# Hybrid decoder layer on one core: masking the decays first, urgent squares and chains, and later first-key products

## The chip, the cores and the metric

The kernel runs on one core of a Trainium2 chip. The metric is device time in microseconds (us), the median of several runs. The profile shows the engines TensorE (PE, with its weight loads PEld), VectorE (DVE), ScalarE (ACT), GpSimd (POOL) and the queue that issues transfers (SP).

## What is computed

One layer on a sequence of 1024 tokens of width 1024. After a norm, one projection gives the columns of two mixers. Mixer A is a gated delta rule with 4 heads of 128 in chunks (the reference's chunk is 64, the kernel's 128); mixer B is dilated window attention with 8 heads of 64. Their outputs are projected and added to the input; a gated MLP with a short convolution and a last norm follow. What the change touches is in mixer A:

```python
qkv_a = jax.nn.silu(causal_dwconv(qkv_a, conv_qkv_w)).astype(jnp.float32)
...
ka = l2norm(ka)
beta = jax.nn.sigmoid(b_a.astype(jnp.float32))
g = -jnp.exp(a_log) * jax.nn.softplus(a_a + dt_bias)
...
gc = jnp.cumsum(chunk_sc(g), axis=-1)
diff = gc[..., :, None] - gc[..., None, :]
dec_incl = jnp.where(incl, jnp.exp(jnp.where(incl, diff, 0.0)), 0.0)
kk = jnp.einsum('nbhtd,nbhjd->nbhtj', kc, kc)
lmat = dec_strict * kk * bc[..., None, :]
...
sol = lax.linalg.triangular_solve(lmat, rhs, left_side=True, lower=True, unit_diagonal=True)
...
def step(state, xs):
    u = uv - jnp.einsum('bhck,bhkv->bhcv', wk, state)
    o = jnp.einsum('bhck,bhkv->bhcv', qd, state) + jnp.einsum('bhcj,bhjv->bhcv', at, u)
    state = ge[..., None, None] * state + jnp.einsum('bhck,bhcv->bhkv', ke, u)
```

## The kernel before

The kernel keeps activations with features on the partitions. A dense product is three matmuls of 128x128x512 on split numbers (`mm3`, with high and low parts), so that a column of 128 output features takes 48 of them. TensorE's order is written by a planner in the kernel, `Weave`: each piece of work is a generator (a stream) with a level; the planner holds an estimated TensorE time `wv.pe` and estimated times at which tiles become ready, takes the stream of the lowest level number among those that are due, and runs it to its next `yield`, whose value says in how many microseconds it wants to go on. `wv.need(tile, slack=...)` is the time until a tile is ready plus a margin; `next_bank("atr")` waits until one of the two result banks of that name is free by the estimates. Each TensorE instruction is stamped, so that TensorE keeps the planner's order exactly. The class `Engine` wraps the other engines: each call adds an estimated duration to the planner's books and then issues the instruction. The order on those engines isn't the planner's; a list scheduler chooses it by readiness and by priority, which follows program order unless it is raised. All their calls pass through one line, so nearly every instruction of VectorE, ScalarE, GpSimd and of the transfer queue has the line L132 in the profile, every matmul L177 and every transpose L181, and groups are told apart by tiles.

The stages, in order of time:

- `first()` multiplies the first three key columns while the input arrives. Beside it, `gates()` multiplies the input by the eight gate columns (`wba`), 8 products for each half, and `norms()` spreads the norm factors `rst` over the partitions into `rstdB` in two halves of transposes. `gates()` ends with the cumulated log decays `gc` and writes them as rows to memory (`gdram`).
- `dense()` multiplies the remaining columns, the fourth key first, then columns of mixer B and the queries and values. It fills whatever the other streams leave free (level 9).
- `first_keys()` and `conv_silu()` turn key columns into keys: three multiply-adds on VectorE, a tanh on ScalarE and a last multiply-add. `kprep(h)` follows for each head: it loads the rows of decays as `dec`, subtracts, masks and exponentiates them, and copies their last column to `gel`; it transposes the keys (`tokens()`, four transposes into each of two `atr` banks), copies them to `ktok` and squares them on ScalarE with a sum for each token (`sq`, sums in `ssk`); and it multiplies keys with keys into `atr` banks, which VectorE takes with `bp` (from `ssk`) and `dec` into `um`.
- After the fourth head, `forward_sub()` solves all 32x32 blocks on VectorE, and `merge()` (two streams of two heads) joins them to 128x128 with small products. `qprep()` and `vprep()` run beside this.
- Four `chain(h)` streams, one for each head, step through eight chunks. A step goes from TensorE to VectorE and back three times: `r`, then `wke`, then the new state (in the tile `ct`), and beside it ScalarE copies `w`, and the output collects in `vtok` with its squares `osq`.
- Attention, output projection, MLP up and down, and the last norm follow. The change doesn't touch them.

The tile for the squares in `tokens()` and the chains has the tag `osq` with one buffer; the tags `w0` to `w3` belong to the chains' `w`. `kprep()` ties `gel` and the decays' first ScalarE pass behind the keys' last operations with order-only dependencies (`after`).

Of the kernel before, what the change touches and what calls it, by code (L numbers as in the profile page):

```python
# [15 lines left out]
P = 128  # L16
# [6 lines left out]
APART = 0.5  # L23
EPS = 1e-6
SLOTS = {"kT": 2, "kU": 2, "dv": 2, "dw": 2, "kt": 4, "uy": 5, "qa": 4, "ev": 2, "go": 2, "Xa": 7, "Xb": 9}
# [91 lines left out]
class Engine:  # L117


    def __init__(self, wv, eng, name, fixed, per, lag=0.28):  # L120
        self.args = wv, eng, name, fixed, per, lag

    def __getattr__(self, op):
        wv, eng, name, fixed, per, lag = self.args

        def call(*a, **kw):
            aps = [x for x in a + tuple(kw.values()) if hasattr(x, "tensor")]
            acc = [kw["accum_out"]] if "accum_out" in kw else []
            n = float(np.prod(aps[0].shape[1:]))
            us = 0.3 + 0.165 * n if kw.get("op") == OP.pow else fixed + per * n  # L130
            wv.account(name, us, aps[:1] + acc, aps[1:], lag)
            return getattr(eng, op)(*a, **kw)  # L132
        return call


def hybrid_layer(tc, I, out):
# [3 lines left out]
    ac = Engine(wv, nc.scalar, "scalar", 0.12, 0.00085)  # L140
    po_ = Engine(wv, nc.gpsimd, "gpsimd", 0.15, 0.0021)
# [191 lines left out]
    def norms():  # L333
        yield wv.need(acc, slack=8.0)
        ssp = yield from next_bank("atr", acc)
        for c in range(NCH):
            mm(ssp[:, c:c + 1], acc[:, c * P:(c + 1) * P], ones[:, :1], 0.215)
            if c % 2:
                yield APART
        ve.tensor_scalar(rst, ssp[:, :NCH], 1.0 / 1024, EPS, op0=OP.mult, op1=OP.add)  # L340
        rsqrt(rst, rst, NCH)
        wv.done.add("rst")
        yield wv.need(rst)
        for h in range(2):
            pb = yield from next_bank("atr")
            for c in range(4):
                i = 4 * h + c
                tp(pb[:, c * P:(c + 1) * P], rst[:, i:i + 1].to_broadcast([P, P]))
            ve.tensor_copy(rstdB[:, half(h)], pb)
        wv.done.add("norms")  # L350
# [154 lines left out]
    def tokens(src, dst, scale=None, ss=None):  # L505

        for hh in range(2):
# [4 lines left out]
            if dst is not None and scale is None:  # L512
                ac.activation(dst[:, half(hh)], pt, AF.Copy)
            for c in range(4):
                i = 4 * hh + c
                if scale is not None:
                    ac.activation(dst[:, i * P:(i + 1) * P], pt[:, c * P:(c + 1) * P], AF.Copy,
                                         scale=scale[:, i:i + 1])
                if ss is not None:
                    sq = tile_(sp, [P, P], F32, "sq", "osq", 1)  # L520
                    ac.activation(sq, pt[:, c * P:(c + 1) * P], AF.Square, accum_out=ss[:, i:i + 1])
        return dst

    def kprep(h):
# [23 lines left out]
        yield wv.need(kT, slack=SLACK)  # L548
# [12 lines left out]
        for c0 in range(0, NCH, 4):  # L561
            pt = yield from next_bank("atr")
# [167 lines left out]
    def chain(h):  # L730
# [14 lines left out]
        for c in range(NCH):  # L745
# [12 lines left out]
            else:  # L758
# [3 lines left out]
                ve.scalar_tensor_tensor(r, ps[:, 0:P], ngam[:, c, h:h + 1], vtok[:, cs], op0=OP.mult, op1=OP.add)  # L762
# [3 lines left out]
            if c < NCH - 1:  # L766
                wke = tile_(sp, [P, P], F32, "wke", "r" + tg, 1)
                ve.tensor_scalar(wke, ps[:, P:2 * P], ke[:, c:c + 1], None, op0=OP.mult)
            ac.activation(w, ps[:, P:2 * P], AF.Copy)
            if c < NCH - 1:  # L770
# [3 lines left out]
                if c == 0:  # L774
                    ve.tensor_copy(sn, ps[:, 2 * P:3 * P])
                else:
                    ve.scalar_tensor_tensor(sn, st, ge[:, c:c + 1], ps[:, 2 * P:3 * P], op0=OP.mult, op1=OP.add)
# [6 lines left out]
            ac.activation(vtok[:, cs], po[:, :P], AF.Copy, scale=rq[:, c:c + 1])  # L784
            if c:
                ve.scalar_tensor_tensor(vtok[:, cs], po[:, P:2 * P], gq[:, c:c + 1], vtok[:, cs], op0=OP.mult,
# [4 lines left out]
            ac.activation(osq, vtok[:, cs], AF.Square, accum_out=ms[:, c:c + 1])  # L791
# [694 lines left out]
```

## Time and profile before

| | us |
|---|---|
| median of 3 runs | 1258.36 |
| lowest, highest | 1257.86, 1259.85 |
| profiled execution | 1259.56 |
| its span | 1257.8 |
| PE busy | 1233.0 |
| DVE busy | 936.0 |
| ACT busy | 621.8 |
| POOL busy | 47.8 |

A timeline row gives start and duration in us, engine, line, operation, output tile and input tiles, the shape, how many instructions are merged, and in square brackets how long the engine had been idle and what ended this. A row of waits gives who waited for whom, the total in us, the number of waits and the longest. Matmuls overlap, so their cost is read from start to start. A matmul of float32 operands is recorded as two instructions, so four products of keys with keys stand as x8.

### The profile page before, as it was taken

How to read it: one execution, taken by the hardware profiler on the slowest of the kernel's cores; microseconds unless marked ns; L12 is line 12 of the kernel's file. 1: busy time of each engine (PE TensorE's matmuls, PEld its weight loads, DVE VectorE, ACT ScalarE, POOL GpSimd, SP SyncE). 2: the span in 40 equal slices, each digit the busy share in tenths (PEclk: the TensorE clock that was granted, in tenths of full speed). 3: DMA queues.
4: the chain of work that ended last, by engine and by line, in shares of the span. 5: the costliest groups of instructions: out<-in, count | busy, mean ns of one | idle time of the engine just before them, and what ended most of it. 6: DMA issues, size and time to landing. Idle time of an engine off the chain costs nothing.

```text
span 1257.8 us, 18320 instructions
## 1 busy us (share of the span) xinstructions
PE 1233.0 (98%) x7040; PEld 1002.1 (80%) x7040; DVE 936.0 (74%) x1462; ACT 621.8 (49%) x1179; POOL 47.8 (4%) x34
## 2 busy tenths in 40 slices
PE   9989999999999999999999999999999999999996
PEld 7768887888676767878788888888888888787886
DVE  7566975563555455676798888888988989899875
ACT  7374444462757374465554454544544454343451
POOL 0021110022000000000000000000000000000000
PEclk9989999999999999999999999999999999999998
DMA  6313244255223420454312313223223298545523
GB/s 228 100 57 94 85 116 137 101 160 206 96 78 100 140 63 26 126 179 139 118 51 101 92 59 101 85 67 101 79 73 101 68 353 290 167 138 198 192 85 134
DMA packets 81974, 153.52 MB, mean 122 GB/s; under 512 B 21824, under 2 KB 32736, under 8 KB 81888
## 3 DMA queue, kind: packets, MB, share of 16 engines
q1 hardware_dynamic: 81888, 152.37, 37.1%
q8 instruction: 55, 0.90, 0.3%
q14 instruction: 31, 0.25, 0.1%
HBM read 114.31 MB, written 35.93 MB: 119 GB/s over the span
## 4 chain that ended last, share of the span: by engine, by line
PE 84%; DVE 7%; DMA 4%; ACT 2%; issue 2%; SPq 0%; POOL 0%; POOLq 0%; DVEq 0%; ACTq 0%
PE ps L177 44%; PE pa L177 18%; PE pc L177 9%; PE dw L177 8%; PE ps L181 4%; DMA wd<-in_wd 3%; DVE pr L132 2%; DVE x1h L132 1%; DVE wd L132 1%; ACT dec L132 1%; DVE kT L132 1%; PE warm L177 1%; DMA wst<-in_wu 0%; DVE r L132 0%; DVE xr L132 0%
## 5 line engine op out<-in xcount | busy, mean ns | idle before, releaser
L177 PE MATMUL dw<-pr 128*128 128x512 f32 (+1 forms) x984 | 213.3, 377 | 2.8 <-DVE x1h L132 2.8
L177 PEld LDWEIGHTS dw<-pr 128*128 128x128 f32 x984 | 176.1, 188 | 38.9 <-DVE x1h L132 4.9
L177 PE MATMUL ps<-xhi,whi 128*128 128x512 f32 x448 | 186.5, 416 | 0.0
L177 PE MATMUL ps<-xhi,wlo 128*128 128x512 f32 x448 | 175.8, 392 | 0.0
L177 PE MATMUL ps<-xlo,whi 128*128 128x512 f32 x448 | 175.3, 391 | 0.0
L177 PE MATMUL pa<-T,pair 128*128 128x512 f32 x528 | 127.1, 389 | 0.6 <-ACT u L132 0.6
L177 PEld LDWEIGHTS pa<-T,pair 128*128 128x128 f32 x528 | 99.0, 188 | 21.1 <-ACT u L132 0.7
L177 PEld LDWEIGHTS ps<-xhi,whi 128*128 128x128 f32 x448 | 84.6, 189 | 19.9 <-issue 6.0
L177 PEld LDWEIGHTS ps<-xhi,wlo 128*128 128x128 f32 x448 | 84.4, 188 | 18.5
L177 PEld LDWEIGHTS ps<-xlo,whi 128*128 128x128 f32 x448 | 84.8, 189 | 13.5
L132 ACT ACTIVATE sm<-sm,mx 128x512 f32<-128x512 f32 (+2 forms) x128 | 79.9, 651 | 23.0 <-DVE mx L132 23.0
L132 ACT ACTIVATE u<-pa 128x512 f32<-128x512 f32 x44 | 26.4, 600 | 110.5 <-PE pa L177 110.5
L132 DVE SCALAR_TENSOR_TENSOR y<-xu,fcw,y 128x1023 f32<-128x1023 f32 (+1 forms) x44 | 56.3, 1281 | 25.7 <-ACT y L132 25.7
L132 ACT ACTIVATE whi<-wst 128x1024 fp32r<-128x1024 f32 (+2 forms) x38 | 38.7, 1017 | 70.4 <-PE ps L177 63.0
L177 PE MATMUL pc<-B,pair 128*128 128x512 f32 x264 | 63.4, 389 | 0.0
L177 PE MATMUL pa<-B,A 128*128 128x512 f32 x264 | 63.4, 389 | 0.0
L177 PE MATMUL pc<-T,S 128*128 128x512 f32 x264 | 63.4, 389 | 0.0
L177 PE MATMUL pa<-T,S 128*128 128x512 f32 x264 | 63.4, 389 | 0.0
L132 ACT ACTIVATE pr<-wd 128x1024 fp32r<-128x1024 f32 x33 | 35.0, 1061 | 55.0 <-DVE wd L132 36.5
L132 DVE TENSOR_TENSOR wst<-wst 128x512 f32<-128x512 f32 x88 | 60.5, 687 | 0.7
L177 PE MATMUL ps<-B,pair 128*128 128x512 f32 x252 | 60.5, 389 | 0.0
L177 PEld LDWEIGHTS pc<-B,pair 128*128 128x128 f32 x264 | 49.6, 188 | 10.3
(230 smaller groups left out, 2279.8 us busy)
## 6 DMA issues: line engine op xcount, KB each, us to landing
wst<-in_wu SPq DMA_DIRECT2D x44, 512.0 KB, 3.7
wd<-in_wd SPq DMA_DIRECT2D x44, 512.0 KB, 4.3
wst<-in_wi SPq DMA_DIRECT2D x25, 512.0 KB, 3.7
upark<-y SPq DMA_DIRECT2D x22, 512.0 KB, 3.7
apark<-aqkv SPq DMA_DIRECT2D x12, 512.0 KB, 2.8
r<-upark SPq DMA_DIRECT2D x11, 512.0 KB, 7.6
r<-upark SPq DMA_DIRECT2D x22, 256.0 KB, 6.7
wa<-in_wd SPq DMA_DIRECT2D x22, 256.0 KB, 2.9
```

The costliest lines, as they stand in the source:

```text
L132: return getattr(eng, op)(*a, **kw)
L177: tc.stamp_issue_order_token(nc.tensor.matmul(dst, lhs, rhs, start=start, stop=stop, **kw).ins, TOKEN)
L181: tc.stamp_issue_order_token(nc.tensor.transpose(dst, src, ident).ins, TOKEN)
```

## The change

- **Decays.** GpSimd's mask (`affine_select`) now comes first, directly on the loaded rows; ScalarE's eight passes by chunk do Exp with the bias instead of Identity, and the separate Exp over 1024 is gone. `gel` is copied after the mask.
- **Priority.** Wrapped engines `uv` and `ua` issue with a priority raised by 400 places. They are used in `tokens()` (copies, scaled copies, squares) and in the four chains.
- **Squares.** The result tiles of the squares in `tokens()` take three tags in turn (`osq`, `w2`, `w3`). The planner's price of a summed Square on ScalarE rises by 0.15 us.
- **Gates.** Each half's eight products are issued in one visit; the pause in the middle moves to the end.
- **Norms.** The second half's spread waits, in the plan, for the first half's copy and 0.3 us.
- **First keys.** For head 0, the transposes are planned 1.5 us later and the first products with themselves 1.0 us later.

```diff
+KSLACK = 1.0
 EPS = 1e-6
+URGENT = 400
...
             us = 0.3 + 0.165 * n if kw.get("op") == OP.pow else fixed + per * n
+            if "func" not in kw and acc and name == "scalar" and a[2] == AF.Square:
+                us += 0.15
             wv.account(name, us, aps[:1] + acc, aps[1:], lag)
-            return getattr(eng, op)(*a, **kw)
+            if first is None:
+                return getattr(eng, op)(*a, **kw)
+            with first(offset=URGENT):
+                return getattr(eng, op)(*a, **kw)
...
+    uv = Engine(wv, nc.vector, "vector", 0.07, 0.00105, first=tc.high_priority)
+    ua = Engine(wv, nc.scalar, "scalar", 0.12, 0.00085, first=tc.high_priority)
...
         for h in range(2):
+            if h:
+                yield wv.need(rstdB, slack=0.3)
             pb = yield from next_bank("atr")
...
                 mm(pt[o:o + 32], wba[:, k, :], xts[k][:, half(h)], 0.23, k < 4, k >= 4, tile_position=(0, o))
-                if k == 3:
-                    yield APART
             ac.activation(barow[:, half(h)], pt, AF.Copy)
-            yield APART
+            yield 2 * APART
...
             if dst is not None and scale is None:
-                ac.activation(dst[:, half(hh)], pt, AF.Copy)
+                ua.activation(dst[:, half(hh)], pt, AF.Copy)
...
                 if ss is not None:
-                    sq = tile_(sp, [P, P], F32, "sq", "osq", 1)
-                    ac.activation(sq, pt[:, c * P:(c + 1) * P], AF.Square, accum_out=ss[:, i:i + 1])
+                    sq = tile_(sp, [P, P], F32, "sq", ("osq", "w2", "w3")[i % 3], 1)
+                    ua.activation(sq, pt[:, c * P:(c + 1) * P], AF.Square, accum_out=ss[:, i:i + 1])
...
+        po_.affine_select(v8(dec), v8(dec), pattern=[[0, NCH], [1, P]], compare_op=OP.is_ge, fill=NEG,
+                                base=0, channel_multiplier=-1)
         late = "the rows may come later than the keys"
         after(ve.tensor_copy(gel, v8(dec)[:, :, P - 1]), kends[h][1], late)
         for c in range(NCH):
-            inst = ac.activation(v8(dec)[:, c, :], v8(dec)[:, c, :], AF.Identity, bias=ngc[:, c, h:h + 1])
+            inst = ac.activation(v8(dec)[:, c, :], v8(dec)[:, c, :], AF.Exp, bias=ngc[:, c, h:h + 1])
             after(inst, kends[h][0], late)
-        po_.affine_select(v8(dec), v8(dec), pattern=[[0, NCH], [1, P]], compare_op=OP.is_ge, fill=NEG,
-                                base=0, channel_multiplier=-1)
         ve.tensor_tensor(gend, gel, gc[:, :, h], op=OP.subtract)
-        ac.activation(dec, dec, AF.Exp)
...
-        yield wv.need(kT, slack=SLACK)
+        yield wv.need(kT, slack=SLACK + 1.5 * (h == 0))
...
-            pt = yield from next_bank("atr")
+            pt = yield from next_bank("atr", slack=KSLACK * (c0 == h == 0))
...
-                ve.scalar_tensor_tensor(r, ps[:, 0:P], ngam[:, c, h:h + 1], vtok[:, cs], op0=OP.mult, op1=OP.add)
+                uv.scalar_tensor_tensor(r, ps[:, 0:P], ngam[:, c, h:h + 1], vtok[:, cs], op0=OP.mult, op1=OP.add)
```

In `chain()` the same replacement of `ve` by `uv` and `ac` by `ua` is made for `wke`, `w`, the state, both writes of `vtok` and `osq`; in `tokens()` also for the scaled copy.

More of the change, by code (lines that the diff above doesn't have):

```diff
@@ L117, with __init__ @@
 class Engine:
-    def __init__(self, wv, eng, name, fixed, per, lag=0.28):
-        self.args = wv, eng, name, fixed, per, lag
+    def __init__(self, wv, eng, name, fixed, per, lag=0.28, first=None):
+        self.args = wv, eng, name, fixed, per, lag, first
     def __getattr__(self, op):
-        wv, eng, name, fixed, per, lag = self.args
+        wv, eng, name, fixed, per, lag, first = self.args
         def call(*a, **kw):
@@ L516, in tokens @@
                 if scale is not None:
-                    ac.activation(dst[:, i * P:(i + 1) * P], pt[:, c * P:(c + 1) * P], AF.Copy,
+                    ua.activation(dst[:, i * P:(i + 1) * P], pt[:, c * P:(c + 1) * P], AF.Copy,
                                          scale=scale[:, i:i + 1])
                 if ss is not None:
-                    sq = tile_(sp, [P, P], F32, "sq", "osq", 1)
-                    ac.activation(sq, pt[:, c * P:(c + 1) * P], AF.Square, accum_out=ss[:, i:i + 1])
+                    sq = tile_(sp, [P, P], F32, "sq", ("osq", "w2", "w3")[i % 3], 1)
+                    ua.activation(sq, pt[:, c * P:(c + 1) * P], AF.Square, accum_out=ss[:, i:i + 1])
         return dst
@@ L767, in chain @@
                 wke = tile_(sp, [P, P], F32, "wke", "r" + tg, 1)
-                ve.tensor_scalar(wke, ps[:, P:2 * P], ke[:, c:c + 1], None, op0=OP.mult)
-            ac.activation(w, ps[:, P:2 * P], AF.Copy)
+                uv.tensor_scalar(wke, ps[:, P:2 * P], ke[:, c:c + 1], None, op0=OP.mult)
+            ua.activation(w, ps[:, P:2 * P], AF.Copy)
             if c < NCH - 1:
@@ L774, in chain @@
                 if c == 0:
-                    ve.tensor_copy(sn, ps[:, 2 * P:3 * P])
+                    uv.tensor_copy(sn, ps[:, 2 * P:3 * P])
                 else:
-                    ve.scalar_tensor_tensor(sn, st, ge[:, c:c + 1], ps[:, 2 * P:3 * P], op0=OP.mult, op1=OP.add)
+                    uv.scalar_tensor_tensor(sn, st, ge[:, c:c + 1], ps[:, 2 * P:3 * P], op0=OP.mult, op1=OP.add)
             yield wv.need(w, qa, slack=HOP)
@@ L782, in chain @@
             mm(po[:, :P], at, w, 0.215)
-            ac.activation(vtok[:, cs], po[:, :P], AF.Copy, scale=rq[:, c:c + 1])
+            ua.activation(vtok[:, cs], po[:, :P], AF.Copy, scale=rq[:, c:c + 1])
             if c:
-                ve.scalar_tensor_tensor(vtok[:, cs], po[:, P:2 * P], gq[:, c:c + 1], vtok[:, cs], op0=OP.mult,
+                uv.scalar_tensor_tensor(vtok[:, cs], po[:, P:2 * P], gq[:, c:c + 1], vtok[:, cs], op0=OP.mult,
                                         op1=OP.add)
@@ L790, in chain @@
             osq = tile_(sp, [P, P], F32, "osq", "osq", 1)
-            ac.activation(osq, vtok[:, cs], AF.Square, accum_out=ms[:, c:c + 1])
+            ua.activation(osq, vtok[:, cs], AF.Square, accum_out=ms[:, c:c + 1])
             wv.done.add(("c", h, c))
```

## The prediction

> **What bounds the kernel now.** I read the shares of busy time, then TensorE's waits by what ended them, then the order of time of TensorE, ScalarE and VectorE round the longest wait.
>
> ```profile
> span 1257.8 us, 18320 instructions
> PE 1233.0 (98%) x7040; PEld 1002.1 (80%) x7040; DVE 936.0 (74%) x1462; ACT 621.8 (49%) x1179; POOL 47.8 (4%) x34
> PE ps L177 <- ACT sq L132: 5.0, 2, 4.4
> PE ps L181 <- DVE rstdB L132: 0.8, 1, 0.8
> PE ps L177 <- DVE vtok L132: 0.7, 1, 0.7
> PE ps L177 <- ACT w L132: 0.5, 1, 0.5
> ```
>
> TensorE is busy for 98% of the span, so time can go only where it stands still or runs slowly. The first wait row (total us, times, longest) is the largest: `mm` waits for ScalarE's squares `sq`, 5.0 us in two waits. No product is removed by the change, so the gain can come only from such waits and from what they bring with them. Here is the longer wait in TensorE's order of time (start, us, instruction, idle before it), with the later products of the same kind for comparison:
>
> ```profile
> 61.12 1.03 PE L181 MATMUL ps<-ident,kT 128*128 128x128 f32 x8
> 66.54 0.39 PE L177 MATMUL ps<-xhi,wlo 128*128 128x512 f32 x1
> 71.35 2.07 PE L177 MATMUL ps<-kT 128*128 128x128 f32 x8 [4.42 <-ACT sq L132]
> 73.08 0.77 PE L177 MATMUL ps<-xhi,whi 128*128 128x512 f32 x1
> 75.78 1.66 PE L177 MATMUL ps<-kT 128*128 128x128 f32 x8
> 77.20 0.48 PE L177 MATMUL ps<-xhi,whi 128*128 128x512 f32 x1
> 80.06 0.60 PE L181 MATMUL ps<-ident,kT 128*128 128x128 f32 x4
> 87.19 1.16 PE L177 MATMUL ps<-kT 128*128 128x128 f32 x8 [0.57 <-ACT sq L132]
> 88.10 0.47 PE L177 MATMUL ps<-xhi,whi 128*128 128x512 f32 x1
> 90.25 1.05 PE L177 MATMUL ps<-kT 128*128 128x128 f32 x8
> 91.06 0.48 PE L177 MATMUL ps<-xhi,whi 128*128 128x512 f32 x1
> ```
>
> The transposes of key head 0 fill both `atr` banks at 61.12. Its first products with themselves need one of these banks back, stand in TensorE's fixed order behind the dense product of 66.54, and start only at 71.35. TensorE then runs slowly for a while. From start to start, the four products take 1.73 us at 71.35 and 1.42 us at 75.78, against 0.91 and 0.81 at 87.19 and 90.25; the six dense products between 73.08 and 75.78 take 2.70 us against 1.43 us for six of the twelve from 77.20 to 80.06 (2.86 us). The excess is 0.82 + 0.61 + 1.27 = 2.70 us. So the place costs 4.42 us of waiting and 2.70 us of slow clock, and its smaller brother another 0.57 us: 7.69 us in all.
>
> By the Trainium skill, page "TensorE: Matmul & The Clock Gate", section "What's actually happening", an idle window of about 3.4 us halves the clock, and about as long a busy one restores it. The trace agrees on the half clock but is slow for 5.85 us (71.35 to 77.20); by the page's 3.4 us the excess would be an estimated 1.7 us, and my gain about 1 us smaller.
>
> Why the bank came late is seen on ScalarE:
>
> ```profile
> 60.33 2.46 ACT L132 ACTIVATE dec<-dec,ngc 128x128 f32<-128x128 f32 x8 [1.38 <-DVE gel L132]
> 62.79 0.58 ACT L132 ACTIVATE ktok<-ps 128x512 f32<-128x512 f32 x1
> 63.27 0.26 ACT L132 ACTIVATE sq<-ps 128x128 f32<-128x128 f32 x1
> 64.10 1.05 ACT L132 ACTIVATE whi<-wst 128x1024 fp32r<-128x1024 f32 x1
> 67.29 1.06 ACT L132 ACTIVATE dec<-dec 128x1024 f32<-128x1024 f32 x1
> 70.93 0.28 ACT L132 ACTIVATE sq<-ps 128x128 f32<-128x128 f32 x1
> 74.15 0.28 ACT L132 ACTIVATE sq<-ps 128x128 f32<-128x128 f32 x1
> 94.33 0.27 ACT L132 ACTIVATE sq<-ps 128x128 f32<-128x128 f32 x1
> 94.72 0.28 ACT L132 ACTIVATE sq<-ps 128x128 f32<-128x128 f32 x1
> ```
>
> The bank's four squares run from 63.27 to 70.93, with weight splits, the next keys' operations and the decays between them; the eighth (the other bank) is at 74.15. Where nothing stands between, two squares start 0.39 us apart (94.33, 94.72). The work for four is thus 1.6 us; the order made it 7.7.
>
> **The change part by part.**
>
> *Squares urgent, three result tiles.* These edits attack that order directly: a ready square goes ahead of the splits and decays, and need not wait for the one tile `osq`. From the end of the transposes, the bank is free after the copy (62.79 to 63.27, 0.48 us) and four squares (1.6 us): 2.1 us, or 3.1 if one 1.05 us operation such as the split has just begun.
>
> *Transposes 1.5 us and first products 1.0 us later in the planner's order.* The transposes come at about 61.12 + 1.5 = 62.6 and end at about 63.4 (0.8 us from start to start of what follows in the plain rows), so the bank is free between 65.5 and 66.5. The first products were due at 66.54 + 0.23 = 66.8. In the new order they can be up to 1.5 + 1.0 + 0.6 us later (the last is four squares at the 0.15 us that the planner now adds), or 1 us earlier, as the decays' long Exp is no longer counted: due between 65.8 and 69.9. Against 65.5 to 66.5 the wait is 0 over most of this and 0.7 us at the worst end. What fills the place are dense products, which must be done anyway, so the delay itself costs TensorE nothing. If that cover were absent, it would cost the 2.5 us by which the two steps are moved.
>
> *What is late next.* The following transposes (80.06) need the banks that VectorE's `um` frees:
>
> ```profile
> 60.13 0.16 DVE L132 COPY gel<-dec 128x8 f32<-128x8 f32 x1
> 75.49 0.17 DVE L132 TENSOR_SCALAR ssk<-ssk 128x8 f32<-128x8 f32 x1
> 78.15 1.12 DVE L132 SCALAR_TENSOR_TENSOR um<-ps,bp,dec 128x128 f32<-128x128 f32 x4
> 83.44 1.12 DVE L132 TENSOR_TENSOR aqkv<-ps,rstdB 128x512 f32<-128x512 f32 x1 [1.70 <-PE ps L177]
> ```
>
> From the sums to the end of `um` it takes 78.15 + 1.12 - 75.49 = 3.8 us, since VectorE's key convolutions go between. With the eighth square done at 65.5 + 2.1 = 67.6, or 1.1 later, `um` ends between 71.4 and 72.5. TensorE reaches the transposes 80.06 - 71.35 - 2.70 = 6.0 us after the first products, at 72.8 if these start at 66.8. That is barely enough; I allow 0.8 us here for small new waits, the size of the row of `rstdB`. The weight split at 64.10 can slip: its column starts only when the one before it ends (83.44 in this trace, some 8 us less after the change), and two or three us of squares don't use that up.
>
> *Decays masked first.*
>
> ```profile
> 62.86 1.10 POOL L132 TENSOR_SCALAR_AFFINE_SELECT dec<-dec 128x1024 f32<-128x1024 f32 x1 [26.69 <-PE ps L177]
> L132 SPq DMA_DIRECT2D dec<-gdram x4: 393/1192/2839, 48.6 to 51.6; - x4
> DMA to landing us min/median/max: 5.5/7.6/8.4
> ```
>
> The eight Identity passes become eight Exp passes with the same bias and shape (2.46 us stays, if Exp costs as Identity does; the long Exp at 1.06 us costs what the split of equal size does at 1.05, so I take them as equal). The Exp over 1024 goes, and its 1.06 us with it, four times, off ScalarE. GpSimd's select moves ahead of `gel`: the first rows land by 48.6 + 8.4 = 57.0 at the latest, the select ends by 58.1, and `gel` starts at 60.13 because of the key before it. So the new wait of `gel` on GpSimd costs nothing, with 2 us in hand; without that cover it would cost up to 1.1 us on VectorE's queue, ahead of the next key. GpSimd has stood idle for 26.69 us at that place, so its queue holds nothing that the select is moved past. The 1.06 us helps ScalarE, which is not the bound once the squares go first: worth 0 to 1.06, taken as 0.
>
> *Norms and gates.*
>
> ```profile
> 25.06 1.06 PE L177 MATMUL ps<-xt,wba 128*32 128x512 f32 x8
> 26.05 0.50 PE L177 MATMUL ps<-xhi,whi 128*128 128x512 f32 x1
> 26.39 0.39 PE L177 MATMUL ps<-xlo,whi 128*128 128x512 f32 x1
> 38.80 0.65 PE L181 MATMUL ps<-ident,rst 128*128 128x128 f32 x4 [0.78 <-DVE rstdB L132]
> ```
>
> The second spread of `rst` now waits in the plan until the first is copied, and dense products fill the 0.78 us: all of it comes back, or none if the plan is off; I take 0.78. For the gates, four visits become two. After a visit the first dense product takes 0.34 us to the next (26.05 to 26.39) where 0.23 is usual, so each avoided visit saves 0.1, or 0.2 with as much at entry; two give 0.2 to 0.4, taken as 0.3.
>
> *Urgent chains.* The chains' operations on VectorE and ScalarE now go ahead of the dense columns' ones in the same queues. TensorE's longest waits for them, on `vtok` and `w`, are 0.7 + 0.5 = 1.2 us. Urgency may remove them, or the new order may add as much: +1.2 to -1.2, taken as 0, since TensorE's own order is fixed by the planner and not by urgency. Behind the urgent operations queue the weight splits and the columns' evacuations, of which each urgent one holds up the next by its own length, some 0.3 us for a quarter of the 1.12 us of `um` above (the same operation on the same shape).
>
> **Sum.** 4.42 + 0.57 + 2.70 + 0.78 + 0.3 = 8.8 us, less 0.8 for small new waits: 8.0 us. The profiled execution took 1259.56 us (span 1257.8 and 1.8 around it), so it would take 1251.6 us. It lay 1.2 us above the median 1258.36, and against the median the forecast is 1250.4 us.
>
> **The rivals.**
>
> *A, a shorter wait stays at the first keys.* For it: the narrow margins above, and that the squares' order is a forecast. Were the squares to stay spread out, so that the change didn't do what it says, the old wait of 4.42 us would still lose the up to 2.1 us by which its product comes later and the 1.06 us of the long Exp. Against it: the work before the bank's release is 2.1 us in rows, and 2.4 us or more are there for it (63.4 to 65.8 or later). Waits of 3 us in all leave a gain of 5.8 us (1252.6), if the clock stays up as it did after 0.57 us; 3.4 us with the slow clock's 2.70 leave 2.7 us (1255.7). Middle: 1254.
>
> *B, the gain is given back before the merges.* The forward substitution on VectorE might not move up with TensorE, and the merges would wait for its loads:
>
> ```profile
> 177.59 4.45 SPq L132 DMA_DIRECT2D um<-xtdram x8
> DMA to landing us min/median/max: 1.8/1.9/4.4
> 188.63 0.69 PE L177 MATMUL ps<-x,um 32*32 32x32 f32 x32
> ```
>
> The loads of the first pair are issued by 182.04 and land 1.8 to 4.4 us later, 2.2 to 4.8 us before they are used. If they didn't move and TensorE came 8.0 us earlier, it would wait 3.2 to 5.8 us, with 2.70 for the clock: 5.9 to 8.5 us back, time 1256.3 to 1258.9, middle 1257.5. Against it: the substitution starts from `um` of the last head, whose products are themselves in TensorE's order and come earlier too.
>
> *C, slower.* The 0.15 us on every square counts for the chains' `osq` too, so the planner, which lets no chain start its next step before `w`, may thin out the chains' products, and VectorE's steps between two of them lie open. Price: one open step is about the 0.7 us of the `vtok` row, and there are three for each of eight chunks, 24 in all, 16.8 us. It decides from 12 open steps (8.0 / 0.7); all 24 give 1250.4 + 16.8 = 1267.2, and 18 give 1263. Against it: dense columns remain as filling, and TensorE's longest waits in that stage are the 1.2 us above.
>
> **How the numbers follow.** Forecast 0.64, A 0.18, B 0.08, C 0.10. A difference below 0.2% (2.5 us) can't be told from none by a measurement of this kernel, whose runs span 2 us. Faster by more than that is below 1255.8: the forecast and nearly all of A, 0.81. B is mostly within it: 0.08. Slower: C and a bit of B, 0.11. The forecast's own range is 1248.4 (no new wait, the chains' 1.2 us gained: 10.0 us) to 1252.6, where A begins. The range goes from 1247, which allows 1.4 us for the spread of the runs, to 1257, through A to the middle of B; it leaves out C, half of B and little more, under 2 in 10.
>
> **What would show it.** Right: no row of TensorE waiting for `sq` above 0.6 us; the squares of a head 0.4 us apart or less with at most one operation between; a granted clock of full speed from 60 to 90 us; four fewer long `dec` Exps; the first merge some 8 us earlier, and all behind it shifted by the same amount. Wrong: a new TensorE wait above 1 us on `um`, `ktok` or `kT` before 100 us (A), on the merges' loads (B), or many short ones on `ct`, `r` and `w` between 220 and 300 us (C).

## The result and the profile after

The changed kernel takes 1248.18 us in the median (1247.26 to 1248.70, four runs); the kernel before took 1258.12 us beside it (1257.86 to 1259.85, four runs). The ratio is 0.9916 (95% interval 0.9904 to 0.9929), so the change gains 9.9 us, or 8.9 to 12.1 by the interval. The forecast was 1250.4. The profiled execution took 1247.26 us, 12.3 less than the one before; that one lay above its median and this one below.

Span, busy time and some of TensorE's waits of the changed kernel (helpers have moved: L187 is a matmul, L191 a transpose; urgent calls have the line L139, the others L137):

```profile
span 1245.0 us, 18305 instructions
PE 1227.5 (99%) x7040; PEld 999.4 (80%) x7040; DVE 939.1 (75%) x1462; ACT 611.4 (49%) x1175; POOL 47.5 (4%) x34
PE ps L187 <- ACT sq L139: 1.0, 2, 0.8
PE ps L187 <- ACT w L139: 0.5, 1, 0.5
PE ps L187 <- DVE ct L139: 0.4, 1, 0.4
PE ps L191 <- POOL vtok L137: 0.3, 1, 0.3
```

The wait for the squares has fallen from 5.0 to 1.0 us, and the row of `rstdB` before a transpose (0.8) is gone. ScalarE has four instructions fewer: the four long Exps. The stretch of the stall, first before and then after (stretch, length, busy time of PE, PEld, DVE, ACT and POOL, then the granted clock, DMA share and GB/s):

```profile
60.00:75.00 15.00, 10.58 (x48) 8.77 (x47) 11.64 (x16) 14.64 (x46) 2.50 (x2) 0.84 0.11 36
75.00:90.00 15.00, 14.43 (x71) 11.95 (x70) 10.16 (x27) 12.42 (x41) 5.80 (x4) 0.93 0.25 79
```

```profile
60.00:75.00 15.00, 15.00 (x76) 12.51 (x75) 13.68 (x20) 14.01 (x52) 1.64 (x1) 1.00 0.13 37
75.00:90.00 15.00, 14.79 (x82) 12.38 (x81) 10.91 (x24) 12.11 (x50) 1.64 (x1) 1.00 0.32 103
```

TensorE now works through at full clock: 158 matmul records stand in these 30 us, where 119 stood. Its order has changed too, which the forecast did not have. TensorE's transposes and key products in order of time, after:

```profile
62.02 1.03 PE L191 MATMUL ps<-ident,kT 128*128 128x128 f32 x8
70.39 0.60 PE L191 MATMUL ps<-ident,kT 128*128 128x128 f32 x4
72.90 0.60 PE L191 MATMUL ps<-ident,kT 128*128 128x128 f32 x4
77.47 1.05 PE L187 MATMUL ps<-kT 128*128 128x128 f32 x8
...
87.37 1.16 PE L187 MATMUL ps<-kT 128*128 128x128 f32 x8 [0.20 <-ACT sq L139]
...
104.29 1.95 PE L187 MATMUL ps<-kT 128*128 128x128 f32 x16
...
118.74 1.16 PE L187 MATMUL ps<-qT,kT 128*128 128x128 f32 x8 [0.82 <-ACT sq L139]
```

Behind the transposes of 62.02 come dense products until 70.39, and then the transposes of head 1, not the products of head 0. Those are the x16 at 104.29, behind the products of all other heads: in the plan, with head 0 held back, head 1's transposes took the `atr` banks as they came free. The last row is the longest wait for squares that is left, 0.82 us before products of queries and keys. ScalarE round head 0's squares:

```profile
65.45 0.57 ACT L139 ACTIVATE ktok<-ps 128x512 f32<-128x512 f32 x1
65.93 0.25 ACT L139 ACTIVATE sq<-ps 128x128 f32<-128x128 f32 x1
66.18 0.26 ACT L139 ACTIVATE sq<-ps 128x128 f32<-128x128 f32 x1
66.43 0.26 ACT L139 ACTIVATE sq<-ps 128x128 f32<-128x128 f32 x1
66.68 1.14 ACT L137 ACTIVATE kT<-xr,gcw 128x1024 f32<-128x1024 f32 x1
67.72 0.58 ACT L139 ACTIVATE ktok<-ps 128x512 f32<-128x512 f32 x1
68.20 0.27 ACT L139 ACTIVATE sq<-ps 128x128 f32<-128x128 f32 x1
```

Three squares stand together, 0.25 us apart, as many as there are result tiles; then a long operation and a copy slip in, and the fourth follows at 68.20. Before, it was at 70.93.

### The profile page after: what moved, and what is told of

Same layout as the page of the kernel before. It is cut to its first block, busy times and chain, and to the rows that moved or that the text cites. A ratio compares the mean times of both kernels' runs of the same rounds, so it can differ in the third digit from the quotient of the medians.

```text
span 1245.0 us, 18305 instructions
## 1 busy us (share of the span) xinstructions
PE 1227.5 (99%) x7040; PEld 999.4 (80%) x7040; DVE 939.1 (75%) x1462; ACT 611.4 (49%) x1175; POOL 47.5 (4%) x34
## 4 chain that ended last, share of the span: by engine, by line
PE 87%; DVE 7%; issue 2%; DMA 2%; ACT 2%; POOL 1%; SPq 0%; POOLq 0%; DVEq 0%; ACTq 0%
PE ps L187 43%; PE pa L187 19%; PE dw L187 12%; PE pc L187 9%; PE ps L191 4%; DVE kT L137 1%; DVE pr L137 1%; DMA wd<-in_wd 1%; DVE x1h L137 1%; PE warm L187 1%; DMA wst<-in_wu 0%; ACT dec L137 0%; DVE aqkv L137 0%; DVE xr L137 0%; ACT sq L139 0%
## 5 line engine op out<-in xcount | busy, mean ns | idle before, releaser
L187 PE MATMUL dw<-pr 128*128 128x512 f32 (+1 forms) x984 | 213.1, 377 | 2.0 <-DVE x1h L137 1.7
L187 PEld LDWEIGHTS dw<-pr 128*128 128x128 f32 x984 | 176.1, 188 | 37.9 <-DVE x1h L137 3.9
L187 PE MATMUL ps<-xhi,whi 128*128 128x512 f32 x448 | 185.5, 414 | 0.0
L187 PE MATMUL ps<-xhi,wlo 128*128 128x512 f32 x448 | 175.3, 391 | 0.0
L187 PE MATMUL ps<-xlo,whi 128*128 128x512 f32 x448 | 175.0, 391 | 0.0
L187 PE MATMUL pa<-T,pair 128*128 128x512 f32 x528 | 127.0, 389 | 0.0
L187 PEld LDWEIGHTS pa<-T,pair 128*128 128x128 f32 x528 | 99.0, 188 | 20.5
L187 PEld LDWEIGHTS ps<-xhi,whi 128*128 128x128 f32 x448 | 84.3, 188 | 19.3 <-issue 5.3
L187 PEld LDWEIGHTS ps<-xhi,wlo 128*128 128x128 f32 x448 | 84.1, 188 | 18.4 <-DVE wlo L137 0.2
L187 PEld LDWEIGHTS ps<-xlo,whi 128*128 128x128 f32 x448 | 84.5, 189 | 13.8 <-DVE xlo L137 0.4
L137 ACT ACTIVATE sm<-sm,mx 128x512 f32<-128x512 f32 (+2 forms) x128 | 79.6, 648 | 22.9 <-DVE mx L137 22.9
L137 ACT ACTIVATE u<-pa 128x512 f32<-128x512 f32 x44 | 26.3, 599 | 110.6 <-PE pa L187 110.6
L137 DVE SCALAR_TENSOR_TENSOR y<-xu,fcw,y 128x1023 f32<-128x1023 f32 (+1 forms) x44 | 56.3, 1281 | 25.7 <-ACT y L137 25.6
L137 ACT ACTIVATE whi<-wst 128x1024 fp32r<-128x1024 f32 (+2 forms) x38 | 38.6, 1017 | 73.4 <-PE ps L187 65.6
L187 PE MATMUL pa<-B,A 128*128 128x512 f32 x264 | 63.4, 389 | 0.0
L187 PE MATMUL pc<-T,S 128*128 128x512 f32 x264 | 63.4, 389 | 0.0
L187 PE MATMUL pa<-T,S 128*128 128x512 f32 x264 | 63.4, 389 | 0.0
L187 PE MATMUL pc<-B,pair 128*128 128x512 f32 x264 | 63.4, 389 | 0.0
L137 DVE TENSOR_TENSOR wst<-wst 128x512 f32<-128x512 f32 x88 | 60.4, 686 | 0.8
L137 ACT ACTIVATE pr<-wd 128x1024 fp32r<-128x1024 f32 x33 | 34.9, 1059 | 52.6 <-DVE wd L137 34.1
L187 PE MATMUL ps<-B,pair 128*128 128x512 f32 x252 | 60.5, 389 | 0.0
L187 PEld LDWEIGHTS pc<-T,S 128*128 128x128 f32 x264 | 49.5, 188 | 10.3
```

What stands on the lines that cost most here:

```text
L187: tc.stamp_issue_order_token(nc.tensor.matmul(dst, lhs, rhs, start=start, stop=stop, **kw).ins, TOKEN)
```

## The experiments

Theory 1 says that the urgency of the squares ends the long wait, Theory 2 that the two delays in the plan end it (the products then come when the bank is free anyway), and Theory 3 that the three result tiles do. Theory 4 puts a part of the gain on the decays, Theory 5 blames the single tile for letting other work in between the squares. Every ratio is to the kernel before, run beside it (medians 1259.86, 1259.55 and 1259.62 us in the three groups). These are some 1.5 us above the 1258.12 us beside the changed kernel, so kernels are best compared by their ratios; the changed kernel's is 0.9916 (0.9904 to 0.9929).

### The changed kernel without the two delays

```diff
-KSLACK = 1.0
+KSLACK = 0.0
-        yield wv.need(kT, slack=SLACK + 1.5 * (h == 0))
+        yield wv.need(kT, slack=SLACK)
```

> The changed kernel, with the first head's two delays in the plan taken back (1.5 and 1.0 us): head 0's products of keys with keys stand again 18 dense products (4.1 us) behind its transposes, not behind the other three heads' products. Theory 1 (urgency ends the wait: copy 0.48 and four squares 1.0 to 1.6 us, plus at most one long operation of 1.05): the bank is free 1.5 to 3.1 us after the transposes, so TensorE waits under 1 us for sq there, and the time is 1248 to 1250 us. Theory 2 (the moved products end the wait, urgency is spare): ScalarE still doesn't reach the squares in time, a wait of 2 us or more with a drop of the granted clock between 60 and 80 us, 1252 to 1256 us.

Measured: 1254.61 us, ratio 0.9950 (0.9934 to 0.9966). Time, wait and clock are those of Theory 2; Theory 1 missed. TensorE, order of time:

```profile
61.76 1.06 PE L191 MATMUL ps<-ident,kT 128*128 128x128 f32 x8 [1.72 <-DVE gel L137]
...
69.33 1.39 PE L187 MATMUL ps<-kT 128*128 128x128 f32 x8 [2.39 <-ACT sq L139]
```

With every square urgent, a wait of 2.39 us for them stays, and the granted clock is 0.89 from 60 to 75 us. A second wait of 1.72 us is new, and it comes from the masked decays. Four of VectorE's multiply-add passes over the first keys, in the kernel before, the changed one, this one, and the changed kernel with the old decays (below):

```profile
52.94 4.86 DVE L132 SCALAR_TENSOR_TENSOR kT<-xr,gcw,kT 128x1023 f32<-128x1023 f32 x4
```

```profile
51.70 6.76 DVE L137 SCALAR_TENSOR_TENSOR kT<-xr,gcw,kT 128x1023 f32<-128x1023 f32 x4
```

```profile
51.60 7.60 DVE L137 SCALAR_TENSOR_TENSOR kT<-xr,gcw,kT 128x1023 f32<-128x1023 f32 x4
```

```profile
51.54 4.86 DVE L137 SCALAR_TENSOR_TENSOR kT<-xr,gcw,kT 128x1023 f32<-128x1023 f32 x4
```

GpSimd's masks now run beside these passes, which take 1.9 to 2.7 us more. The first key's last pass starts at 59.65 us in the changed kernel and at 60.39 here, against 57.58 with the old decays, and the transposes, which the plan here does not hold back, wait for it. With the delay of 1.5 us they do not.

### The kernel before with the two delays alone

```diff
-        yield wv.need(kT, slack=SLACK)
+        yield wv.need(kT, slack=SLACK + 1.5 * (h == 0))
...
-            pt = yield from next_bank("atr")
+            pt = yield from next_bank("atr", slack=1.0 * (c0 == h == 0))
```

> The kernel before, with nothing but the first head's two delays in the plan (1.5 and 1.0 us): head 0's products come behind those of the other three heads. Theory 1 (urgency is needed): the squares of the other heads are as spread out as head 0's were, so one of them keeps TensorE waiting 2 us or more; 1253 to 1257 us. Theory 2 (the moved products suffice): no wait for sq above 1 us and full clock from 60 to 90 us; 1249 to 1251.5 us (7.7 us off 1258.1, less nothing for norms and gates).

Measured: 1263.70 us, ratio 1.0027 (1.0016 to 1.0039), 3.4 us slower, which neither theory had foreseen. TensorE, and the same stretch by windows:

```profile
79.68 1.12 PE L181 MATMUL ps<-ident,kT 128*128 128x128 f32 x4 [4.79 <-ACT sq L132]
```

```profile
75.00:90.00 15.00, 10.32 (x43) 8.68 (x44) 8.99 (x20) 13.14 (x48) 5.83 (x4) 0.77 0.20 70
```

The wait has not gone; it has moved. Head 1's second transposes want the same bank and stand 4.79 us, with the clock at 0.77 from 75 to 90 us. A second wait for squares, of 2.39 us, stands later, before products of queries and keys. Theory 2 falls: the delays do not help while the squares are spread out.

### The kernel before with urgent squares and three tiles

```diff
+    ua = Engine(wv, nc.scalar, "scalar", 0.12, 0.00085, first=tc.high_priority)
...
-                    sq = tile_(sp, [P, P], F32, "sq", "osq", 1)
-                    ac.activation(sq, pt[:, c * P:(c + 1) * P], AF.Square, accum_out=ss[:, i:i + 1])
+                    sq = tile_(sp, [P, P], F32, "sq", ("osq", "w2", "w3")[i % 3], 1)
+                    ua.activation(sq, pt[:, c * P:(c + 1) * P], AF.Square, accum_out=ss[:, i:i + 1])
```

The copies in `tokens()` are made urgent in the same way.

> The kernel before, with urgent copies and squares of the transposed keys, queries and values and three result tiles, TensorE's order as before. Theory 1: the eight squares of head 0 take 2 to 4 us instead of 11, the wait of 4.4 us falls below 1 us, no slow clock: 1250 to 1251.5 us. Theory 2: other work that stands ahead on ScalarE (decays, key 1's tanh, a weight split) still delays them; a wait of 2 us or more stays: 1254 to 1257 us.

Measured: 1254.05 us, ratio 0.9953 (0.9940 to 0.9965): 5.9 us of the 9.9. The first products wait 1.00 us for the squares, the next transposes 0.95 us for `um`, and the clock stays at 1.00. The wait is near what Theory 1 expected, the time is not: it lies just inside Theory 2's range, without Theory 2's wait.

### The changed kernel with plain calls in tokens()

```diff
-                    ua.activation(sq, pt[:, c * P:(c + 1) * P], AF.Square, accum_out=ss[:, i:i + 1])
+                    ac.activation(sq, pt[:, c * P:(c + 1) * P], AF.Square, accum_out=ss[:, i:i + 1])
```

Its copies are plain too.

> The changed kernel without urgency in the tokens' copies and squares (chains stay urgent, three tiles stay); TensorE's order is that of the changed kernel. Theory 1: the squares spread out again, and one of heads 1 to 3 or head 0 keeps TensorE waiting 2 us or more: 1251 to 1256 us. Theory 2: within 0.1% of the changed kernel (1247 to 1249.5 us), as every product stands far enough behind its squares.

Measured: 1250.05 us, ratio 0.9918 (0.9903 to 0.9932), the changed kernel's own 0.9916. The waits for `sq` are 1.3 us in two. The median lies 0.55 us above Theory 2's range, but by the ratio the two kernels can't be told apart: the urgency of the squares can be left out.

### The same with one result tile

```diff
-                    sq = tile_(sp, [P, P], F32, "sq", ("osq", "w2", "w3")[i % 3], 1)
+                    sq = tile_(sp, [P, P], F32, "sq", "osq", 1)
```

> The changed kernel with plain tokens and also with one result tile for the squares, so that of the edits at the keys only the delays in the plan, the price of a square and the decays' new form are left. Theory 3 (the three tiles, not urgency, let squares stand together): squares are spread over ScalarE's queue again, TensorE waits 2 us or more for sq, 1252 to 1260 us. Theory 4 (the decays' lost Exp and the order of the products leave ScalarE time enough): no wait for sq above 1.5 us, 1247.5 to 1250.5 us.

Measured: 1253.28 us, ratio 0.9951 (0.9937 to 0.9964), 4 us worse than with three tiles. The longest of its waits for `sq`, which are 4.9 us in five (3.1 before products, 1.8 before transposes), and the squares of head 0's first bank on ScalarE:

```profile
72.12 0.66 PE L191 MATMUL ps<-ident,kT 128*128 128x128 f32 x4 [1.66 <-ACT sq L137]
```

```profile
66.75 0.26 ACT L137 ACTIVATE sq<-ps 128x128 f32<-128x128 f32 x1
68.52 0.27 ACT L137 ACTIVATE sq<-ps 128x128 f32<-128x128 f32 x1
71.31 0.27 ACT L137 ACTIVATE sq<-ps 128x128 f32<-128x128 f32 x1
71.70 0.28 ACT L137 ACTIVATE sq<-ps 128x128 f32<-128x128 f32 x1
```

With one tile the first and the second square each have long operations behind them, as before the change: from the first to the fourth it takes 4.95 us, against 2.27 above. The time is Theory 3's; the longest wait, 1.66 us, lies between what the two theories expected.

### The kernel before with three tiles alone

```diff
-                    sq = tile_(sp, [P, P], F32, "sq", "osq", 1)
+                    sq = tile_(sp, [P, P], F32, "sq", ("osq", "w2", "w3")[i % 3], 1)
```

> The kernel before with three result tiles for the squares and nothing else; no urgency, TensorE's order as before. Theory 5 (the single tile is what let other work in between the squares; urgency adds little): the wait of 4.4 us at head 0 falls below 2 us and the clock stays up, 1251 to 1254.5 us, near the 5.9 us that urgency and tiles gave together. Rival (urgency did it): the wait stays above 3 us, 1256 to 1259.5 us.

Measured: 1254.39 us, ratio 0.9963 (0.9951 to 0.9976). TensorE:

```profile
68.40 1.16 PE L177 MATMUL ps<-kT 128*128 128x128 f32 x8 [1.00 <-ACT sq L132]
...
75.53 0.66 PE L181 MATMUL ps<-ident,kT 128*128 128x128 f32 x4 [0.95 <-DVE um L132]
```

Both waits are those of the kernel with urgency, to 0.01 us. TensorE's order is unchanged, and one changed line has taken the 4.42 us to 1.00 and kept the clock up: Theories 3 and 5 hold, and the urgency isn't needed for it. Its squares start at 63.72, 63.97 and 64.22, and the fourth at 67.98: three together, then, among others, a copy, a split and two of the next keys' operations.

### The kernel before with the delays and three tiles

This is the edit of the delays and that of the tiles together.

> The kernel before with the first head's two delays in the plan and three result tiles. The delays alone made TensorE wait 4.8 us for head 0's squares at head 1's transposes and cost 3.4 us. Theory 5: with the tiles this wait falls below 2 us, 1252 to 1256 us. Rival (the decays' old form or the missing price of a square is to blame): the wait stays above 3 us, 1257 us or more.

Measured: 1255.06 us, ratio 0.9968 (0.9957 to 0.9980). The 4.79 us before head 1's transposes are gone, but the later wait, before products of queries and keys, is still there (2.39 us with the delays alone):

```profile
120.38 3.11 PE L177 MATMUL ps<-qT,kT 128*128 128x128 f32 x16 [2.11 <-ACT sq L132]
```

On the kernel before, the delays add nothing to the tiles.

### The changed kernel with four tiles

```diff
-                    sq = tile_(sp, [P, P], F32, "sq", ("osq", "w2", "w3")[i % 3], 1)
+                    sq = tile_(sp, [P, P], F32, "sq", ("osq", "w1", "w2", "w3")[i % 4], 1)
```

> The changed kernel with four result tiles instead of three, one for each square of a bank; TensorE's order is that of the changed kernel. Theory 5: with three tiles three squares stand together and the fourth lets one long operation in; with four, a bank's four squares stand together, and the waits for sq (1.0 us) go: 1247 to 1249 us, 0 to 1 us faster than the changed kernel. Rival: no difference at all in the waits, as other things set them.

Measured: 1250.25 us, ratio 0.9928 (0.9914 to 0.9941), no gain over three. The squares start together, at 66.74, 66.99, 67.24 and 67.48, so the number of tiles does set the group. But the waits for `sq` have not gone; they are 2.0 us in two, and a later head's products wait longer than the changed kernel's 0.20 us:

```profile
88.30 1.16 PE L187 MATMUL ps<-kT 128*128 128x128 f32 x8 [1.14 <-ACT sq L139]
```

The changed kernel with plain chains (below), on three tiles and in the same order, waits 1.00 us for the same products, so the fourth tile need not be the reason.

### Four tiles, with the transposes delayed and the products not

```diff
-KSLACK = 1.0
+KSLACK = 0.0
```

> The changed kernel with four result tiles and without the 1.0 us at head 0's first products (the 1.5 us at its transposes stay): its products stand 34 dense products (7.7 us) behind its transposes, before head 1's transposes. Theory (the forecast's picture: the bank is free within some 3 us of the transposes, so the products need not go behind the other heads): no wait for sq above 0.6 us, 1247 to 1249.5 us, as the changed kernel. Rival (the late products carry part of the gain): a wait of 1 us or more on um or sq before 100 us, 1250 us or more.

Measured: 1250.25 us, ratio 0.9924 (0.9910 to 0.9938). Head 0's products are back in their place, at 70.33 and ahead of head 1's transposes, and wait for nothing; 0.75 us is lost at 77.61. The time is that of four tiles with the products last, so their place is worth nothing that these runs can tell. Time and wait are a little above what the theory expected, and the wait is below the rival's.

### The changed kernel with the old decays

```diff
-        po_.affine_select(v8(dec), v8(dec), pattern=[[0, NCH], [1, P]], compare_op=OP.is_ge, fill=NEG,
-                                base=0, channel_multiplier=-1)
...
-            inst = ac.activation(v8(dec)[:, c, :], v8(dec)[:, c, :], AF.Exp, bias=ngc[:, c, h:h + 1])
+            inst = ac.activation(v8(dec)[:, c, :], v8(dec)[:, c, :], AF.Identity, bias=ngc[:, c, h:h + 1])
...
+        po_.affine_select(v8(dec), v8(dec), pattern=[[0, NCH], [1, P]], compare_op=OP.is_ge, fill=NEG,
+                                base=0, channel_multiplier=-1)
+        ac.activation(dec, dec, AF.Exp)
```

> The changed kernel with the decays in their old form (Identity by chunk, mask, Exp over 1024). Theory 3: urgent squares on three tiles are in time with or without it; within 0.2% of the changed kernel, 1247.5 to 1251 us. Theory 4: ScalarE has 1.06 us more for each head ahead of the squares, and GpSimd's mask stands in the way of um; a wait of 1.5 us or more, 1251 to 1256 us.

Measured: 1251.01 us, ratio 0.9938 (0.9922 to 0.9954). The interval overlaps the changed kernel's, and TensorE's order differs (head 0's products come before the last head's). No wait for `sq` is left in it, while waits on `um`, `vT` and "issue" of 0.9, 0.7 and 0.8 us are new. Inconclusive: the decays are worth between nothing and some 3 us, and Theory 4 stays open.

### The changed kernel with plain chains

```diff
-                uv.scalar_tensor_tensor(r, ps[:, 0:P], ngam[:, c, h:h + 1], vtok[:, cs], op0=OP.mult, op1=OP.add)
+                ve.scalar_tensor_tensor(r, ps[:, 0:P], ngam[:, c, h:h + 1], vtok[:, cs], op0=OP.mult, op1=OP.add)
...
```

> The changed kernel with plain chains; TensorE's order is that of the changed kernel. Forecast: urgency there is worth nothing, within 0.1% (1247.5 to 1250 us). Rival: it is worth the waits on vtok and w that it was to end, some 1.2 us (1249.5 to 1251.5 us), with these rows back among TensorE's waits.

Measured: 1249.32 us, ratio 0.9922 (0.9909 to 0.9934). The rows of `w`, `ct` and `vtok` read 0.5, 0.4 and 0.3 us as in the changed kernel. Urgency in the chains does nothing that these runs can tell.

### The changed kernel with the old norms and gates

```diff
-            if h:
-                yield wv.need(rstdB, slack=0.3)
...
+                if k == 3:
+                    yield APART
...
-            yield 2 * APART
+            yield APART
```

> The changed kernel with the norms' and gates' edits undone. Forecast: 0.78 us of waiting for rstdB and about 0.3 us of switching come back: 1.1 us slower, 1249 to 1250.5 us. Rival: what they save is lost again at a later wait, and the time is that of the changed kernel within 0.5 us.

Measured: 1251.80 us, ratio 0.9937 (0.9925 to 0.9949). The first and last of its four gate visits, and its second spread:

```profile
25.75 1.06 PE L187 MATMUL ps<-xt,wba 128*32 128x512 f32 x8
...
32.19 1.06 PE L187 MATMUL ps<-xt,wba 128*32 128x512 f32 x8
...
39.48 0.65 PE L191 MATMUL ps<-ident,rst 128*128 128x128 f32 x4 [0.78 <-DVE rstdB L137]
```

and the two visits of the changed kernel:

```profile
25.55 1.92 PE L187 MATMUL ps<-xt,wba 128*32 128x512 f32 x16
...
28.98 1.92 PE L187 MATMUL ps<-xt,wba 128*32 128x512 f32 x16
```

The 0.78 us is back. From the first gate product to head 0's transposes (at 63.85 here) with 120 dense products in each it takes 38.10 us, against 62.02 - 25.55 = 36.47: 1.63 us, of which 0.78 is the wait and 0.85 is left for the two visits saved. The time is above both expectations. By the ratios the edits are worth 2.6 us, in intervals that overlap; beyond the 1.63 us the profile has longer waits for `sq`, `u` and `xlo` (0.6, 0.8 and 0.4 us more), which differ between the other profiles too.

No version tried beat the changed kernel.

## Why the prediction was right, and where it was not

**The cause of the stall** was read rightly: a bank held by four squares spread over 7.7 us. Drawn together they ended the wait, with one line (three tiles alone).

**What draws them together** was put half wrong. The step named the urgency first and the single tile beside it. The tiles are enough: three tiles without urgency give the waits of both, and the changed kernel runs as fast without the squares' urgency or without the chains' as with them. Urgency on one tile was not tried, so what it would do alone stays open. The groups of three and four in the rows show the number of tiles at work. The reason is argued and not shown by itself: with one tile, each square must end before the list scheduler finds the next one ready, and ready long operations were put between.

**When the bank comes free** was put at 65.5 to 66.5. The fourth square starts at 68.20, so it was about 68.5: the urgent copy stood behind a split and a key operation until 65.45, and a long operation and a copy still followed the third square. Had the products been due at 65.8 to 69.9, as forecast, up to 2.7 us of waiting would have been left. The run without delays shows such a wait: 2.39.

**Where the delays put the products** was wrong. They went to 104.29, not to some place up to 69.9, since the step reckoned the delay in time but not that head 1's transposes, which got no delay, could take the banks first. So the bank's next user came at 70.39, behind its release, and its lateness did no harm. The run with the products in their old place shows that the far place was not needed: with four tiles and the transposes alone held back, the products come at 70.33, wait for nothing, and the time is the same. In both, the next user came later than the forecast's 65.8 to 69.9, as the bank did: two errors of the step offset each other, and that no wait was left at this place was in part luck.

**Masking first at no cost** was wrong by 1.9 us of VectorE's time, the difference of the x4 rows. The forecast looked at GpSimd's queue and at the select's end, not at VectorE's passes beside it. What covers it is the delay of the transposes by 1.5 us; without that cover TensorE waits 1.72 us, and the forecast's price for the cover gone was at most 1.1 us. The Trainium skill, page "SBUF — State Buffer", section "Who interferes with whom", says that a VectorE instruction with two SBUF inputs contends with a GpSimd instruction that reads SBUF; the rows agree, both engines being slower together (the select's row stands in the last section).

**"The first merge 8 us earlier, and all behind it shifted equally"** was wrong. These are TensorE's first merge product, a late product of attention and the first of the MLP, after the change, then two of them before (the first merge was at 188.63):

```profile
194.87 0.69 PE L187 MATMUL ps<-x,um 32*32 32x32 f32 x32
...
481.39 1.92 PE L187 MATMUL ps<-pb,vc 128*64 128x128 f32 x32
...
607.25 2.97 PE L187 MATMUL pa<-T,pair 128*128 128x512 f32 x12
```

```profile
491.43 1.92 PE L177 MATMUL ps<-pb,vc 128*64 128x128 f32 x32
...
617.98 3.02 PE L177 MATMUL pa<-T,pair 128*128 128x512 f32 x12 [0.58 <-ACT u L132]
```

The merges come 6.2 us later, not 8 us earlier, and attention still ends 10.0 and the MLP starts 10.7 us earlier. In between, the time won was spent on dense columns: 675 dense products stand ahead of the first merge, where 618 stood. At some 0.23 us each, the 57 more are about 13 us of work done earlier, which is then missing as filling later, so it was only moved. The forward substitution starts no earlier (115.2 us, against 115.4), as rival B supposed, but nothing waited for it, because TensorE had other work. In the kernel with three tiles alone the shift is what the step said:

```profile
183.32 0.69 PE L177 MATMUL ps<-x,um 32*32 32x32 f32 x32
...
485.85 1.92 PE L177 MATMUL ps<-pb,vc 128*64 128x128 f32 x32
...
612.07 3.01 PE L177 MATMUL pa<-T,pair 128*128 128x512 f32 x12 [0.19 <-ACT u L132]
```

Here they are 5.3, 5.6 and 5.9 us earlier.

**The sum, term by term** (us):

| term | forecast | measured |
|---|---|---|
| waits for the squares | 4.42 + 0.57 | 5.0 - 1.0 = 4.0 |
| slow clock | 2.70 | 2.70 (the forecast's figure, as the clock is 1.00 from 60 to 90 us) |
| norms' wait | 0.78 | 0.78 |
| gates | 0.3 | 0.85 |
| other small waits to the end of attention | -0.8 | +0.8 |
| sum | 8.0 | 9.1 |

The last term is the rows of `vtok` (0.7), `ot`, `pb`, `mx` and `ct` (0.2 each) before, 1.5 us, against `vtok` (0.3) and `ct` (0.4) after. It was the largest miss: the allowance for new waits was not used, since their place went to dense products. Of the gain of 9.9 us some 0.8 has no row, which is within the interval. The profiled pair differs by 2.4 us more than the medians. Of that, 1.7 are the waits on `x1h` and `u` in the MLP (3.4 before, 1.7 after); in the other kernels' profiles the two add up to between 2.4 and 3.5 whatever the edit, so they are put down to the execution and not to the change.

**The signs.** The full clock from 60 to 90 us and the four Exps came as the forecast said, and none of the signs against it did. Three of its own did not come: TensorE still waits 1.0 us for squares, 0.82 at the longest where 0.6 was allowed; two operations and not one stand between the third and the fourth square; and the merges come later.

**The rivals.** A, a shorter wait that stays, is what three tiles alone and the changed kernel without delays gave (1254.39 and 1254.61, forecast 1254); in the changed kernel it is avoided, and with the old decays too. Delays and tiles alone still had 2.11 us before the products of queries and keys, where the changed kernel has 0.82. Without the norms' and gates' edits the same products wait 0.82 us as well, and without the squares' urgency too, so none of these is needed to end the longer wait. The planner's higher price of a square is left, or several edits together; the price was not tried alone, and this stays open. C did not come: the chains' waits on `vtok`, `w` and `ct` fell from 1.4 to 1.2 us.

## What to carry to other kernels

Before raising the priority of small operations that come out spread, count their result tiles: at the first head here as many as there are tiles were issued together, and the priority on top did nothing. A delay written into one stream of a planned order also hands its buffers to the streams that have none, so ask who takes them; alone, it only moved the wait and cost 3.4 us. And time won on the busiest engine is kept if there is filling work, even when the dependent chain behind it comes no earlier.

## What the runs showed of the hardware

- A GpSimd select beside VectorE's multiply-adds slows both. Three selects took 6.18 us together after the change, while one alone took 1.10 before; the four passes on VectorE took 6.76 us instead of 4.86. Which of the two pays differs: in the run with one tile the four selects took 1.10, 1.09, 1.27 and 1.80 us, and four passes 7.71.

```profile
53.23 6.18 POOL L137 TENSOR_SCALAR_AFFINE_SELECT dec<-dec 128x1024 f32<-128x1024 f32 x3 [1.09 <-DMA dec<-gdram]
```

- The clock falls after shorter waits than the forecast's rival A assumed (3.4 us). It fell behind waits of 2.39 us (without delays, 0.89 from 60 to 75 us) and of 2.11 us (delays and tiles, where 120 to 125 us read 0.66), and it stayed at 1.00 behind 1.72 us (without delays, the first wait), 1.66 us (one tile) and 1.00 us (three tiles alone). The Trainium skill, page "TensorE: Matmul & The Clock Gate", section "What's actually happening", gives about 3.4 us of idleness; these two waits are shorter, and here the measurement decides.

```profile
120.00:125.00 5.00, 4.62 (x21) 4.22 (x22) 5.00 (x14) 1.36 (x11) 1.65 (x1) 0.66 0.33 105
```

- The length of a wait doesn't settle it alone. At the last norm TensorE waits 2.10 us for `rstdB` in all fourteen profiles here. At the end of this wait the clock is already at half in the kernel before and with four tiles; in the other twelve it is still full, and stays so for about half a microsecond or more.

- Once at half, the clock stayed there for about 3.4 us or twice that. In steps of 0.1 us it reads 1.00 or 0.50, but for the steps at the edges, so a mean tells how long it was low: 0.66 over 5 us (delays and tiles) is 3.4 us at half, and 0.89 over 15 us (without delays) is 3.3; 0.77 over 15 us (delays alone), and 0.84 and 0.93 over the two 15 us of the kernel before, are 6.9 each. The prediction's 5.85 us of slow products are the part of this last stretch in which TensorE had work.

- Squares that stand together start 0.25 us apart when they write to different tiles, against 0.39 on one tile.
